# Four edits to the issue order of a four-branch encoder layer: a time-step load as one row, head weights split tile by tile, one attention stage in source order, U weights loaded ahead

## The chip, the cores and the metric

The kernel runs on one core of one Trainium2 chip. The metric is the device time of one execution in microseconds (us). The core has five engines with instruction streams of their own: TensorE (PE in the rows; its weight loads are PEld), VectorE (DVE), ScalarE (ACT), GpSimd (POOL) and SyncE (SP), which here only issues DMAs. Each engine takes its instructions strictly in their order and waits at semaphores for the others. ACT and POOL can issue DMAs too.

## The reference, cut to what matters

One residual layer over x (2048 tokens, 1024 channels), all in float32. One input projection feeds four branches; each branch is gated by a SiLU path, projected, and merged by sigmoid gates before one output projection.

```python
h = rms_norm(x, norm_g)
proj = einsum('bsd,dc->bsc', h, w_in)                 # 1024 x 10240
a_out = s5_branch(ssm_u, ..., log_dt, ...)            # diagonal state space; dt = exp(log_dt), 32 groups
b_out = retention(q, k, v)                            # 4 heads, chunks of 64
c_out = diff_attention(q, k, v)                       # 4 heads, two softmaxes each, blocks of 128 queries
m_out = memory_attention(q, mem)                      # 4 heads, 256 memory tokens
x = x + (sum_n sigmoid(merge_n + b_n) * (branch_n * silu(gate_n)) @ w_branch_n) @ w_out
```

## The kernel before

The sequence is worked in two blocks of 1024 tokens, `b` = 0 and 1. Each block runs these stages one after the other: retention (`retention_branch`; in block 0 its `side` also holds the norms of x, the S5 tables and the memory keys), differential attention (`diff_branch`), the Strassen-like projections (`projections`), merge, and output. In the trace, retention of block 0 runs from about 30 to 370 us, its attention to 680, its projections to 1160, merge and output to 1510; block 1 takes the rest.

A float32 product is made of three float32r matmuls (`mm3`, L74 to L76): weights and activations are split into a high part (a cast on ACT, names ending in h) and a low part (a subtraction on POOL or DVE, names ending in l). The splits of weights are thus work for ACT, POOL and DVE that has to be ready when PE wants it. `load_w512` loads and splits the eight 128x512 tiles of one head's query, key, value and gate weights, `w5h` and `w5l`; even tiles are subtracted on POOL, odd ones on DVE. The raw tiles `w_r` have four buffers.

Inside retention and attention the order of the work is written with `Events`: each step of each unit (a head `h` and a tile `t` of 128 tokens, 32 units for each block) gets a time in units, and the steps are emitted sorted by that time. A Tile scheduler then reorders the emitted instructions on each engine by its own estimate of when they are ready, with the emitted order as priority. One unit of attention passes through `queries`, `score` (PE scores, DVE maximum, ACT exponential `pr`), `weights_a` and `weights_b` (the coefficients `cf`), `mix` (DVE, and ACT for odd chunks, combine the two softmaxes into one `pr`), `turn` (PE transposes of `pr` into `tr`, an ACT copy to `at`), `values` (PE, `o<-vt,at`), `finish` (an ACT scaling `on` by `rms_r`, which POOL computes) and `store`. The projection of a unit that comes `lead` units later is spread between them in eight steps of three matmuls. In the last `lead` units, where no projection is left, `tail` puts the projection of the S5 input U there instead (`s5_input`): four column tiles `e`, each with weights of two 128x512 pieces that are loaded and split (`w1h`, `w1l`) at the start of its first half.

In retention a unit is `project`, `scale`, `turn`, `score` (PE, then DVE masks into `rsm`), `values` (PE, L919 to L922), `finish` and `store`.

The first DMAs of the program are, on SP, `n_x` (x, tile 0), `n_g` (the norm's gain, spread to all partitions), `n_x` (tile 1), four `w_r`, `rdec`, `n_x` (tile 2), four more `w_r`; and, on ACT, two that bring `log_dt` into `ldt`, whose source pattern steps over every second float:

```python
A.dma_start(out=ldt[g2 * 64:(g2 + 1) * 64, :],
            in_=bass.AP(src.tensor, src.offset + g2, [[0, 64], [2, NPAIR]]))
```

`ldt` is needed by `setup_s5` alone, whose first step is `dt` on POOL.

Of the kernel before, what the change touches and what calls it, by code (L numbers as in the profile page):

```python
# [15 lines left out]
ALU = mybir.AluOpType  # L16
# [27 lines left out]
def trunk_kernel(ctx, tc, a):  # L44
    nc = tc.nc
    V, A, G, PE, DMA = nc.vector, nc.scalar, nc.gpsimd, nc.tensor, nc.sync

# [94 lines left out]
    def setup_vectors(p):  # L142
# [18 lines left out]
        V.tensor_scalar(HEAD_G, HEAD_G, 0.5 * (1.0 - LAMBDA_INIT), None, op0=ALU.mult)  # L161
        lt = p.tile([128, 4, 64], F32, name="lt")
# [284 lines left out]

    def raw_w128(src):
# [187 lines left out]
    def diff_branch(b, wp, close_w, tail):  # L636
# [6 lines left out]
        with pool("diff", side="right") as p:  # L643

            def project(h, t):
                st = heads[h]
                if t == 0:
                    st["w"] = w_in512(wp, DQ_C, h)
# [20 lines left out]
                yield from proj_nat(o, b, t, st["w"])  # L669
# [153 lines left out]
            dense = []  # L823

            def start_tail():
                close_w()
                dense.append(tail())

            for i, u in enumerate(units):
# [8 lines left out]
                for c in range(n):  # L838
                    at(i + 1.22 + lag + 0.9 * c / n, x.mix, c)
                    at(i + (1.57, 1.52)[b] + lag + 0.9 * c / n, x.turn, c)  # L840
                    at(i + (1.85, 1.77)[b] + lag + 0.9 * c / n, x.values, c)
                at(i + 2.8 + lag, x.finish)
                if x.t % 4 == 3:
                    at(i + 3.3 + lag, x.store)
# [17 lines left out]
    class Ret:  # L862


        w, raws = {}, {}
# [4 lines left out]
        def project(self):  # L870
            b, h, t, p = self.b, self.h, self.t, self.p
            if t == 0:
# [6 lines left out]
            yield from proj_nat(o, b, t, Ret.w[h])  # L879
# [64 lines left out]
    def retention_branch(b, wp, side):  # L944
        with pool("ret") as p, ExitStack() as wx2:
# [6 lines left out]
            for i, (h, t) in enumerate((h, t) for h in range(NH) for t in range(8)):  # L952
# [5 lines left out]
                events.at(i + 3.3, x.values)  # L958
                events.at(i + 4.1, x.finish)
                if t % 4 == 3:  # L960
                    events.at(i + 4.7, x.store)
# [6 lines left out]
    def s5_input(b, e, w1, up):  # L968
# [610 lines left out]
    for b in range(NBLK):  # L1579
# [4 lines left out]
        if b == 0:  # L1584
            with ExitStack() as sx:
# [116 lines left out]
```

## Time and profile before

| what | value |
|---|---|
| runs | 3047.42, 3050.52, 3054.89 us, median 3050.52 us |
| the profiled execution | 3045.78 us, span of its instructions 3043.5 us |
| PE busy | 2899.1 us, 95% of the span |
| DVE, ACT, POOL busy | 1920.5, 1332.3, 1247.0 us |
| granted clock of TensorE, mean | 0.99 |
| moved by DMA | 351.75 MB |

The profiled execution is 4.7 us below the median. A busy PE is not PE at its peak: a matmul counts as busy until its modelled end, which overlaps the next one. An idle time is put down to the engine and the line that ended it.

### The profile page before, as it was taken

Reading aid. Unit: us, or ns where it says so; the run is one execution under the profiler, and the core shown is the slowest. Engines: PE = TensorE matmul, PEld = TensorE weight load, DVE = VectorE, ACT = ScalarE, POOL = GpSimd, SP = SyncE. Lnnn points to the kernel's source line nnn. Section 1 sums busy time; section 2 is a strip of 40 time slices with the busy share of each in tenths; the row PEclk is TensorE's granted clock in tenths of the full one; section 3 lists DMA queues with packets and bytes.
Section 4 is the critical chain, followed back from the end, with each engine's and each line's share of the span. In section 5 each row is a group of like instructions: output and inputs, shape, how many; then the busy total and the mean of one; then the engine's idle time right before and its main releaser. Section 6 shows DMA issues by size and latency. Waiting matters only on the chain. (4 is left out here: it accounts for less than half of the span.)

```text
span 3043.5 us, 43500 instructions
## 1 busy us (share of the span) xinstructions
PE 2899.1 (95%) x14514; PEld 2381.9 (78%) x14514; DVE 1920.5 (63%) x4613; ACT 1332.3 (44%) x3357; POOL 1247.0 (41%) x1157
## 2 busy tenths in 40 slices
PE   5999999998999999999999999999999999999999
PEld 4777877777888888777788878878878888887777
DVE  5885587766655545656544378888766555446654
ACT  3323355563333344423433257767733333444332
POOL 2543533334444442555132242232244444434560
PEclk9999999999999999999999999999999999999999
DMA  5332422233444436555521220120134444355653
GB/s 154 97 92 77 126 68 68 68 97 119 141 150 142 134 109 204 188 182 175 161 69 43 63 66 22 58 61 21 59 115 142 144 142 137 125 184 166 194 167 96
DMA packets 319341, 351.75 MB, mean 116 GB/s; under 512 B 28479, under 2 KB 238478, under 8 KB 319118
## 3 DMA queue, kind: packets, MB, share of 16 engines
q1 hardware_dynamic: 314734, 340.59, 35.7%
q0 software_dynamic: 2304, 8.39, 0.9%
q8 instruction: 114, 1.87, 0.3%
q14 instruction: 109, 0.89, 0.1%
q10 hardware_dynamic: 2080, 0.01, 0.0%
HBM read 247.98 MB, written 100.93 MB: 115 GB/s over the span
## 5 line engine op out<-in xcount | busy, mean ns | idle before, releaser
L1294 POOL TENSOR_TENSOR p_l<-p_r,p_h 128x512 fp32r<-128x512 f32 x260 | 368.4, 1420 | 458.3 <-ACT p_h L1293 445.3
L74 PE MATMUL mm<-w5h,xh 128*128 128x512 f32 x1024 | 436.3, 426 | 17.9 <-ACT xh L577 16.5
L75 PE MATMUL mm<-w5l,xh 128*128 128x512 f32 x1024 | 406.7, 397 | 3.5 <-POOL w5l L443 3.5
L76 PE MATMUL mm<-w5h,xl 128*128 128x512 f32 x1024 | 406.9, 397 | 0.0
L138 POOL TENSOR_TENSOR rms_r<-rms_m,mhalf 128x1 f32<-128x1 f32 (+1 forms) x228 | 179.0, 787 | 488.2 <-DVE rms_m L136 422.6
L1293 ACT CAST p_h<-p_r 128x512 fp32r<-128x512 f32 x260 | 160.3, 621 | 376.6 <-PE mm L1332 85.8
L758 ACT ACTIVATE pr<-sc,nm 128x512 f32<-128x512 f32 (+3 forms) x320 | 200.1, 626 | 148.0 <-DVE nm L756 146.4
L74 PEld LDWEIGHTS mm<-w5h,xh 128*128 128x128 f32 x1024 | 195.2, 191 | 48.3 <-ACT xh L577 16.9
L76 PEld LDWEIGHTS mm<-w5h,xl 128*128 128x128 f32 x1024 | 194.2, 190 | 43.9
L75 PEld LDWEIGHTS mm<-w5l,xh 128*128 128x128 f32 x1024 | 195.8, 191 | 32.1 <-POOL w5l L443 4.7
L75 PE MATMUL sc<-br_l,w1h 128*128 128x512 f32 x496 | 197.3, 398 | 6.9 <-DVE br_l L1212 6.9
L74 PE MATMUL sc<-br_h,w1h 128*128 128x512 f32 x496 | 200.5, 404 | 3.3 <-DVE mg_g L1265 3.3
L756 DVE TENSOR_REDUCE nm<-sc 128x1 f32<-128x512 f32 (+3 forms) x320 | 193.2, 604 | 9.3 <-PE sc L752 5.1
L76 PE MATMUL sc<-br_h,w1l 128*128 128x512 f32 x496 | 197.3, 398 | 0.0
L1266 POOL TENSOR_TENSOR mg<-mg,mg_g 128x512 f32<-128x512 f32 x96 | 140.9, 1471 | 91.9 <-DVE mg_g L1265 83.8
L806 PEld LDWEIGHTS o<-vt,at 128*128 128x128 f32 x1088 | 142.4, 193 | 38.0 <-ACT at L799 29.6
L806 PE MATMUL o<-vt,at 128*128 128x128 f32 x1088 | 152.0, 279 | 16.6 <-ACT at L799 16.5
L460 POOL TENSOR_TENSOR w1l<-w_r,w1h 128x512 fp32r<-128x512 f32 x86 | 119.4, 1401 | 113.3 <-ACT w1h L459 95.8
L443 POOL TENSOR_TENSOR w5l<-w_r,w5h 128x512 fp32r<-128x512 f32 x72 | 96.0, 1336 | 109.9 <-ACT w5h L442 73.7
L1332 PE MATMUL mm<-xh,p_h 128*128 128x512 f32 x336 | 134.0, 399 | 0.3 <-ACT p_t L1402 0.3
L1332 PE MATMUL sc<-xl,p_h 128*128 128x512 f32 x336 | 131.6, 392 | 2.7 <-DVE xl L1367 2.7
L1332 PE MATMUL sc<-xh,p_h 128*128 128x512 f32 x336 | 131.3, 391 | 0.6 <-ACT p_h L1293 0.6
(396 smaller groups left out, 7653.6 us busy)
## 6 DMA issues: line engine op xcount, KB each, us to landing
p_r<-in_w_in SPq DMA_DIRECT2D x88, 512.0 KB
w_r<-in_w_in SPq DMA_DIRECT2D x144, 256.0 KB
me_d<-p_t SPq DMA_DIRECT2D x128, 256.0 KB
mg_g<-me_d SPq DMA_DIRECT2D x64, 512.0 KB
s_m<-mats_d SPq DMA_DIRECT2D x32, 640.0 KB
w_r<-in_w_branch SPq DMA_DIRECT2D x64, 256.0 KB
w_r<-br SPq DMA_DIRECT2D x64, 256.0 KB
n_x<-in_x SPq DMA_DIRECT2D x16, 512.0 KB
```

The costliest lines, as they stand in the source:

```text
L74: PE.matmul(out, l[0], r[0], start=first, stop=False)
L75: PE.matmul(out, l[0], r[1], start=False, stop=False)
L76: PE.matmul(out, l[1], r[0], start=False, stop=last)
L138: G.tensor_tensor(r, m, mhalf[:, 0:n], op=ALU.pow)
L460: G.tensor_tensor(lo, raw, hi.bitcast(F32), op=ALU.subtract)
L756: V.tensor_reduce(nm, s[:, 0:n], axis=AX.X, op=ALU.max, negate=True)
L758: A.activation(e[:, 0:n], s[:, 0:n], AF.Exp, bias=nm, accum_out=self.zz[:, m, c:c + 1])
L806: PE.matmul(self.o[:, 0:128], self.at[c][:, q * 128:(q + 1) * 128], self.st["vts"][c][:, q, :], start=c == 0 and q == 0, stop=c * 4 + q == ...
L1266: G.tensor_tensor(dst, dst, t, op=ALU.add)
L1293: A.copy(hi, x)
L1294: G.tensor_tensor(lo, x, hi.bitcast(F32), op=ALU.subtract)
L1332: PE.matmul(o, l[:, k, :], r, start=first and k == 0 and q == 0, stop=k == 3 and q == 2, skip_group_check=True)
```

## The change

1. `log_dt` is loaded as one contiguous row of 32 floats, spread to all partitions, by an SP DMA in `setup_vectors` (after the first x tiles and weights), and two DVE copies pick the even and the odd entries into `ldt`. The two ACT DMAs at the program's start go.
2. `w512_steps` splits a head's weights one tile for each step, within the last projection steps of the head before (and, in attention, the first of its own head), in place of `w_in512` in one piece at the head's first tile. The first head of each stage, and in block 1 retention's first head, still load in one piece.
3. The whole attention stage of block 0 (`events.run()` with b = 0) is issued on DVE, ACT, POOL and PE in the order of the source, without the scheduler's reordering. Block 1 is still scheduled.
4. U weights: the pieces of column tile e + 1 are requested when tile e begins and split after its first half; those of tile 0 are requested 0.7 unit before the tail and split when it begins. The tail's steps come three eighths of a unit later.
5. Some times in `Events` move: attention's `values` from 1.85 to 1.95 (block 0) and 1.77 to 1.82 (block 1), `finish` and `store` a little later; retention's `values` from 3.3 to 3.6, `finish` from 4.1 to 4.4, `store` from 4.7 to 5.0.

```diff
@@ setup_vectors
+        row = p.tile([128, NPAIR, 2], F32, name="ldt_r")
+        DMA.dma_start(out=row.rearrange("p j g -> p (j g)"), in_=a["ssm_log_dt"][0].partition_broadcast(128))
+        for g2 in range(2):
+            V.tensor_copy(ldt[g2 * 64:(g2 + 1) * 64, :], row[g2 * 64:(g2 + 1) * 64, :, g2])
@@ new
+    def w512_steps(p, src, w):
+        raws = [raw_w512(src, k) for k in range(4)]
+        yield
+        for k in range(8):
+            raw = raws.pop(0)
+            hi = p.tile([128, 512], F32R, name="w5h", bufs=8)
+            lo = p.tile([128, 512], F32R, name="w5l", bufs=8)
+            A.copy(hi, raw)
+            (V if k % 2 else G).tensor_tensor(lo, raw, hi.bitcast(F32), op=ALU.subtract)
...
+            if k < 4:
+                raws.append(raw_w512(src, k + 4))
+            yield
@@ diff_branch, project
-                if t == 0:
-                    st["w"] = w_in512(wp, DQ_C, h)
+                if t == 7 and h + 1 < NH:
+                    heads[h + 1]["w"] = [], []
+                    heads[h + 1]["ws"] = w512_steps(wp, cols512(DQ_C, h + 1), heads[h + 1]["w"])
...
-                yield from proj_nat(o, b, t, st["w"])
+                groups = proj_nat(o, b, t, st["w"])
+                for k in range(8):
+                    if t == 0 and h and k < 5:
+                        next(st["ws"])
+                    if t == 7 and h + 1 < NH and k in (1, 5, 6, 7):
+                        next(heads[h + 1]["ws"])
+                    next(groups, None)
+                    if k < 7:
+                        yield
@@ diff_branch, events
-                    at(i + (1.85, 1.77)[b] + lag + 0.9 * c / n, x.values, c)
+                    at(i + (1.95, 1.82)[b] + lag + 0.9 * c / n, x.values, c)
...
+                        at(i - 0.7, lambda: ahead.append([raw_u(0, k) for k in range(2)]))
                         at(i, start_tail)
                     for k in range(8):
-                        at(i + (k + 0.5) / 8, lambda: next(dense[0], None))
-            events.run()
+                        at(i + (k + 3.5) / 8, lambda: next(dense[0], None))
+            with ExitStack() as ox:
+                if b == 0:
+                    ox.enter_context(tc.manual_schedule(engines=ORDERED))
+                events.run()
@@ Ret.project
-                if h or b:
-                    Ret.w[h] = w_in512(self.wps[h % 2], RQ_C, h, Ret.raws.pop(h, ()))
+                if h == 0 and b:
+                    Ret.w[h] = w_in512(self.wps[0], RQ_C, h, Ret.raws.pop(h, ()))
...
+                if t == 6 and k == 1 and h + 1 < NH:
+                    Ret.w[h + 1] = [], []
+                    Ret.ws = w512_steps(self.wps[(h + 1) % 2], cols512(RQ_C, h + 1), Ret.w[h + 1])
+                    next(Ret.ws)
+                if t == 7 and h + 1 < NH:
+                    next(Ret.ws)
@@ retention_branch
-                events.at(i + 3.3, x.values)
+                events.at(i + 3.6, x.values)
@@ s5_input
-        w = w_in128(w1, U_C + e * 128)
+        w = ws.pop(e)
+        if e < 3:
+            raws = [raw_u(e + 1, k) for k in range(2)]
...
+            if hf == 0 and e < 3:
+                ws[e + 1] = s5_weights(w1, raws)
@@ block 0, before the norms
-                for g2 in range(2):
-                    src = a["ssm_log_dt"]
-                    A.dma_start(out=ldt[g2 * 64:(g2 + 1) * 64, :],
-                                in_=bass.AP(src.tensor, src.offset + g2, [[0, 64], [2, NPAIR]]))
```

The order of instructions shows what moves. First POOL at the start of the program, where `dt` stood ahead of the first split of weights. Before:

```order
L138 TENSOR_TENSOR rms_r<-rms_m,mhalf 128x1
L194 TENSOR_TENSOR dt<-ebase,ldt 128x16
L443 TENSOR_TENSOR w5l<-w_r,w5h 128x512
L138 TENSOR_TENSOR rms_r<-rms_m,mhalf 128x1
L443 TENSOR_TENSOR w5l<-w_r,w5h 128x512
```

And in the changed program, the same engine from the same place on:

```order
L139 TENSOR_TENSOR rms_r<-rms_m,mhalf 128x1
L448 TENSOR_TENSOR w5l<-w_r,w5h 128x512
L139 TENSOR_TENSOR rms_r<-rms_m,mhalf 128x1
L448 TENSOR_TENSOR w5l<-w_r,w5h 128x512
L139 TENSOR_TENSOR rms_r<-rms_m,mhalf 128x1
L448 TENSOR_TENSOR w5l<-w_r,w5h 128x512 x2
L943 TENSOR_TENSOR rqk<-ram,rbm 128x256
L139 TENSOR_TENSOR rms_r<-rms_m,mhalf 128x1
L943 TENSOR_TENSOR rqk<-ram,rbm 128x256
L199 TENSOR_TENSOR dt<-ebase,ldt 128x16
L207 TENSOR_TENSOR mag<-ebase,t_872 128x16
L175 TENSOR_TENSOR ls<-eb,ls 128x2
```

`dt` has moved behind the first splits and the first two retention units, to just ahead of `mag`.

Second ACT in block 0's attention, where the weights of the second head are split. Before:

```order
L442 CAST w5h<-w_r 128x512 x2
L799 COPY at<-tr 128x512
L442 CAST w5h<-w_r 128x512
L758 ACTIVATE pr,zz<-sc,nm 128x256
L442 CAST w5h<-w_r 128x512
L629 ACTIVATE ho_j,ho_ss<-o 128x128
L442 CAST w5h<-w_r 128x512
L740 CAST qh<-tr 128x256
L633 ACTIVATE on<-on,rms_r 128x128
L442 CAST w5h<-w_r 128x512
L799 COPY at<-tr 128x128
L442 CAST w5h<-w_r 128x512
```

In the changed program, the same place:

```order
L829 COPY at<-tr 128x512
L788 ACTIVATE pr,zz<-sc,nm 128x256
L650 ACTIVATE ho_j,ho_ss<-o 128x128
L770 CAST qh<-tr 128x256
L461 CAST w5h<-w_r 128x512
L788 ACTIVATE pr,zz<-sc,nm 128x256
L829 COPY at<-tr 128x128
L461 CAST w5h<-w_r 128x512 x2
L701 COPY raw<-mm 128x256
L702 COPY vt<-mm 128x128
L632 ACTIVATE si_t<-mm 128x128
L654 ACTIVATE on<-on,rms_r 128x128
```

Six casts stood ahead of the small `at` copy, and `on` with them; now one cast does, and `on` comes behind the copy.

Third PE at that same unit: from the transpose of `pr` to the product `o<-vt,at` that uses its copy. Before:

```order
L797 MATMUL tr<-ident,pr 128x128
L74 MATMUL mm<-w5h,xh 128x512
L75 MATMUL mm<-w5l,xh 128x512
L76 MATMUL mm<-w5h,xl 128x512
L74 MATMUL mm<-w5h,xh 128x512
L75 MATMUL mm<-w5l,xh 128x512
L76 MATMUL mm<-w5h,xl 128x512
L806 MATMUL o<-vt,at 128x128
```

In the changed program:

```order
L827 MATMUL tr<-ident,pr 128x128
L75 MATMUL mm<-w5h,xh 128x512
L76 MATMUL mm<-w5l,xh 128x512
L77 MATMUL mm<-w5h,xl 128x512
L75 MATMUL mm<-w5h,xh 128x512
L76 MATMUL mm<-w5l,xh 128x512
L77 MATMUL mm<-w5h,xl 128x512
L75 MATMUL mm<-w5h,xh 128x512
L76 MATMUL mm<-w5l,xh 128x512
L77 MATMUL mm<-w5h,xl 128x512
L836 MATMUL o<-vt,at 128x128
```

One more group of three projection matmuls now stands between the transpose and its use.

## Rows read from the trace of the kernel before

**Rows 1.** Stretches: PE, PEld, DVE, ACT, POOL busy us, granted clock, DMA share, GB/s.

```profile
500.00:600.00 100.00, 92.94 (x511) 76.67 (x510) 79.73 (x245) 57.41 (x182) 39.39 (x57) 1.00 0.21 65
900.00:1000.00 100.00, 100.00 (x488) 81.81 (x487) 52.59 (x108) 39.09 (x67) 43.75 (x33) 1.00 0.47 151
```

**Rows 2.** Timeline of the start: start us, us, what [idle before it <- releaser].

```profile
2.26 19.86 SPq L432 DMA_DIRECT2D w_r<-in_w_in  x4
4.32 1.06 ACT L565 ACTIVATE n_junk<-n_x 128x1024 bf16<-128x1024 f32 x1 [0.80 <-DMA n_x<-in_x]
26.15 1.06 ACT L565 ACTIVATE n_junk<-n_x 128x1024 bf16<-128x1024 f32 x1 [20.68 <-DMA n_x<-in_x]
26.50 2.91 POOL L194 TENSOR_TENSOR dt<-ebase,ldt 128x16 f32<-128x16 f32 x1 [20.20 <-DMA ldt<-in_ssm_log_dt]
29.25 0.62 ACT L442 CAST w5h<-w_r 128x512 fp32r<-128x512 f32 x1 [0.22 <-DMA w_r<-in_w_in]
29.38 1.27 POOL L443 TENSOR_TENSOR w5l<-w_r,w5h 128x512 fp32r<-128x512 f32 x1
30.41 0.79 PE L74 MATMUL mm<-w5h,xh 128*128 128x512 f32 x1 [16.50 <-ACT xh L577]
34.73 1.12 PE L574 MATMUL tr<-ident,n_x 128*128 128x128 f32 x4 [3.10 <-DVE xl L578]
```

**Rows 3.** DMA queues: 0 to 40 us, then 10 to 15 us (q10 ACT's, q1 SP's): packets, MB, share.

```profile
q10 hardware_dynamic: 2080, 0.01, 2.4%
...
q10 hardware_dynamic: 547, 0.00, 4.8%
q1 hardware_dynamic: 3, 0.00, 0.2%
```

**Rows 4.** Stretches of the start and of slow clocks, columns as in rows 1.

```profile
2.00:4.00 2.00, 0.00 (x0) 0.00 (x0) 0.30 (x1) 1.28 (x1) 0.00 (x0) 1.00 0.83 252
36.00:40.00 4.00, 4.00 (x17) 3.38 (x16) 3.92 (x4) 2.57 (x5) 3.21 (x3) 1.00 1.04 338
102.50:106.00 3.50, 3.50 (x10) 2.43 (x9) 3.35 (x12) 1.14 (x4) 2.02 (x2) 0.51 0.71 212
460.00:464.40 4.40, 3.88 (x12) 3.21 (x13) 3.12 (x11) 2.92 (x11) 2.08 (x3) 0.61 0.86 260
2130.00:2150.00 20.00, 16.84 (x86) 13.62 (x86) 14.80 (x39) 11.43 (x31) 8.54 (x9) 0.91 0.34 106
```

**Rows 5.** Waits of PE, 40 to 110, then 60 to 380 us: us in total, times, longest.

```profile
PE tr L574 <- DVE rms_m L136: 2.7, 1, 2.7
...
PE sc L919 <- DVE rsm L911: 5.4, 5, 3.0
```

**Rows 6.** Waits of PE from 380 to 740 us (attention, block 0, and after).

```profile
PE o L806 <- ACT at L799: 12.5, 15, 3.0
...
PE tr L797 <- DVE kt L714: 3.0, 4, 1.3
PE tr L797 <- DVE sc L754: 1.9, 4, 0.5
```

**Rows 7.** Timeline of the longest of these waits: ACT, then PE.

```profile
459.39 0.40 ACT L633 ACTIVATE on<-on,rms_r 128x128 f32<-128x128 f32 x1 [1.02 <-POOL rms_r L138]
460.21 0.26 ACT L799 COPY at<-tr 128x128 f32<-128x128 f32 x1
...
460.51 0.49 PE L806 MATMUL o<-vt,at 128*128 128x128 f32 x2 [3.00 <-ACT at L799]
```

**Rows 8.** Waits of PE: 1790 to 2260 us (attention, block 1), then 2120 to 2150 us.

```profile
PE o L806 <- ACT at L799: 4.0, 7, 0.7
...
PE mm L76 <- POOL w1l L460: 0.6, 1, 0.6
...
PE tr L797 <- DVE pr L790: 2.9, 2, 2.5
```

**Rows 9.** Waits of PE from 1480 to 1790 us (retention, block 1), the first.

```profile
PE mm L75 <- POOL w5l L443: 3.5, 3, 2.3
```

More of the change, by code (lines that the diff above doesn't have):

```diff
@@ L46, in trunk_kernel @@
     V, A, G, PE, DMA = nc.vector, nc.scalar, nc.gpsimd, nc.tensor, nc.sync
+    ORDERED = {x.engine for x in (V, A, G, PE)}
     def pool(name, bufs=1, side=None, space=None):
@@ L446, in load_w512 @@
         return his, los
+    def w512_steps(p, src, w):
[7 more added lines that the diff above has]
+            (V if k % 2 else G).tensor_tensor(lo, raw, hi.bitcast(F32), op=ALU.subtract)
+            w[0].append(hi)
+            w[1].append(lo)
+            if k < 4:
+                raws.append(raw_w512(src, k + 4))
+            yield
     def raw_w128(src):
@@ L633, in head_scale, with diff_branch @@
         A.mul(on, on, r)
-    def diff_branch(b, wp, close_w, tail):
+    def diff_branch(b, wp, close_w, tail, ahead):
         nkv, npr = ((4, 12), (6, 14))[b]
@@ L823, in diff_branch @@
             dense = []
+            heads[0]["w"] = w_in512(wp, DQ_C, 0)
             def start_tail():
@@ L827, in start_tail @@
                 dense.append(tail())
+                next(dense[0])
             for i, u in enumerate(units):
@@ L862, in trunk_kernel @@
     class Ret:
-        w, raws = {}, {}
+        w, raws, ws = {}, {}, None
         def __init__(self, b, h, t, wps, p, rtab, rmask):
@@ L875, in project @@
                     DMA.dma_start(out=state[h], in_=state_d[:, h, :])
-                if h or b:
-                    Ret.w[h] = w_in512(self.wps[h % 2], RQ_C, h, Ret.raws.pop(h, ()))
+                if h == 0 and b:
+                    Ret.w[h] = w_in512(self.wps[0], RQ_C, h, Ret.raws.pop(h, ()))
             o = ps_mm()
-            yield from proj_nat(o, b, t, Ret.w[h])
+            groups = proj_nat(o, b, t, Ret.w[h])
+            for k in range(8):
+                if t == 6 and k == 1 and h + 1 < NH:
[4 more added lines that the diff above has]
+                    next(Ret.ws)
+                next(groups, None)
+                if k < 7:
+                    yield
             qk = o[:, 0:256].rearrange("p (a d) -> p a d", a=2)
@@ L957, in retention_branch @@
                 events.at(i + 2.7, x.score)
-                events.at(i + 3.3, x.values)
-                events.at(i + 4.1, x.finish)
+                events.at(i + 3.6, x.values)
+                events.at(i + 4.4, x.finish)
                 if t % 4 == 3:
-                    events.at(i + 4.7, x.store)
+                    events.at(i + 5.0, x.store)
                 if i == 6:
@@ L965, in retention_branch, with raw_u, s5_weights, s5_input @@
             events.run()
-    def s5_input(b, e, w1, up):
-        w = w_in128(w1, U_C + e * 128)
+    def raw_u(e, k):
+        return raw_w128(w_in[k * 512:(k + 1) * 512, U_C + e * 128:U_C + (e + 1) * 128])
+    def s5_weights(w1, raws):
+        return [load_w128(w1, None, raw, bufs=4) for raw in raws]
+    def s5_input(b, e, ws, w1, up):
+        w = ws.pop(e)
+        if e < 3:
+            raws = [raw_u(e + 1, k) for k in range(2)]
         us = up.tile([128, 8, 128], F32, name="us", bufs=1)
@@ L1636, in tail @@
             with pool("us") as up:
+                ws = {0: s5_weights(w1, ahead.pop(0))}
+                yield
                 for e in range(4):
@@ L1639, in tail @@
                         ahead[0].load()
-                    yield from s5_input(b, e, w1, up)
-        dense = diff_branch(b, wp, wx.close, tail)
+                    yield from s5_input(b, e, ws, w1, up)
+        dense = diff_branch(b, wp, wx.close, tail, ahead)
         drain(dense)
```

4 lines of the change are left out of this document (2 added, 2 removed).

## Prediction, made before the changed kernel ran

> **What bounds the kernel now.** I read the stretches of 100 us first, because an average over stages says little here. In the projections PE is busy for the whole stretch; in attention of block 0 it is idle for 7 of 100 us while no other engine is full [rows 1]. PE busy 2899.1 us of a span of 3043.5 us leaves about 144 us of PE idle in the whole program, and that is all that a change of order can win directly; nothing here shortens a matmul. So the question for each edit is which of PE's waits it ends, and I read PE's waits stage by stage.
>
> The largest is at the start. PE's first projection matmul comes at 30.41 us after an idle time of 16.50 us [rows 2]. It hangs on ACT, which stood 20.68 us for `n_x` (tile 1), a transfer that SP had requested before 2.26 us. The reader is to see three things together: SP needed 19.86 us to issue four `w_r` [rows 2]; from 10 to 15 us ACT's queue sent 547 packets and SP's three [rows 3]; and POOL's `dt`, which waits for `ldt` itself, began at 26.50 us, right after `n_x` had come [rows 2]. The 2,080 packets of `ldt` carry 0.01 MB [rows 3]. I take it that this load, one packet for each float, holds up everything queued beside it until it is through.
>
> A second fact makes long waits dearer: after the wait of 3.00 us at 460.51 us [rows 7] the granted clock of the stretch is 0.61, a mixture of 2.4 and 1.2 GHz, and after the 3.0 us wait in retention it is 0.51 [rows 4, 5]. A stretch at half clock loses half its length: 4.4 x 0.39 = 1.7 us and 3.5 x 0.49 = 1.7 us.
>
> **The start (edit 1).** With `ldt` gone, what has to land before the first matmul after tile 0 (landed at 4.32 us [rows 2]) is `n_g` and `n_x` of 512 KB each and four `w_r` of 256 KB: 2048 KB, 2.10 million bytes. SP's loads moved 252 GB/s before `ldt` began to count, and 338 GB/s later [rows 4]: 8.3 or 6.2 us, so the last `w_r` lands at 12.6 or 10.5 us. Before, the first matmul followed the start of the fourth cast, which waited for that `w_r`, by 30.41 - 29.25 = 1.16 us [rows 2]. It comes at 13.8 or 11.7 us, 16.6 or 18.7 us earlier. Beyond that, POOL's first `w5l` had to stand behind `dt` until 29.38 us, and the second four `w_r` could be requested only when it was done; the 3.10 us wait at 34.73 us [rows 2] follows from this crowding and may go too. Bounds 16.6 to 21.8; I take **-17**, because the wait at 34.73 is for DVE, whose own list is unchanged.
>
> The new row load is one more SP issue after the first weights; it is wanted by `dt` alone. But `dt`'s 2.91 us of POOL [rows 2] now lie ahead of `mag`, `ls` and the norms' `rms_r`, in a place where PE already waited 2.7 us for that chain [rows 5], and on DVE two copies and the product with `dt` stand ahead of an `xl`. Between 0 and 2.9 us; I take half, **+1.5**.
>
> **Retention, block 0 (edits 2 and 5).** PE waits 5.4 us in five places for `rsm` (DVE) before `values` [rows 5], and one of them brings 1.7 us of half clock. `values` comes 0.3 of a unit later, two groups of three projection matmuls by the order. A stretch of attention holds 511 matmuls in 100 us [rows 1], so a matmul is some 0.2 us apart from the next (an estimate) and six give 1.2 us. That covers the four shorter waits, which hold 2.4 us, and shortens the 3.0 us one, perhaps below the point where the clock falls. Bounds 0 to -7.1; I take **-5**. The splits of heads' weights cost nothing here either way: the waits for `w5l` are 3.5 us in block 1's retention and all belong to its first head, which still loads in one piece [rows 9]: **0**.
>
> **Attention, block 0 (edits 2, 3 and 5).** 12.5 us in 15 waits of `values` for the `at` copy [rows 6]. The longest shows why: the small copy at 460.21 us had stood on ACT behind casts of the next head's weights and behind `on`, which itself stood 1.02 us for POOL's `rms_r` [rows 7], and POOL was splitting the same weights. In the changed order one cast stands ahead of this copy, `on` behind it, and PE has one more group of three matmuls, some 0.6 us, to work on first. The longest is gone twice over; most others are below 1 us, the size of what the later time gives. With the half clock after the longest the bounds are 0 and -14.2; I take **-10**. The source order also moves ACT's and DVE's share of `mix`. The transposes' waits of 3.0 and 1.9 us [rows 6] could shrink by that or double, so 4.9 us either way; I take **0**.
>
> **Attention, block 1, and both tails (edits 4 and 5).** Block 1's `values` waits hold 4.0 us [rows 8], and 0.05 of a unit is about 0.7 us there, as long as the longest of them. Between 2120 and 2150 us the transposes wait 2.9 us for `pr`, 2.5 of it at once [rows 8], while POOL splits two U pieces at a time and DVE waits for POOL; the clock of that stretch, 0.91 over 20 us [rows 4], costs 1.8 us. Splitting the pieces half a column tile ahead takes this apart. Together 0 to -8.3; I take **-5**. The waits for `w1l` of 0.6 us [rows 8], in each block one: **-1**.
>
> **The sum.** -17 + 1.5 - 5 - 10 - 5 - 1 = -36.5 us against the profiled execution: 3045.8 - 36.5 = **3009 us**. That execution lies 4.7 us below the median of the runs, so the same gain from the median would give 3014; I stay with the profiled sum, since a PE that waits less should also vary less, and put the difference into the range. All bounds at their best give 3045.8 - 21.8 - 7.1 - 14.2 - 4.9 - 8.3 - 1.2 = 2988; the start at its least, `dt` at its dearest, nothing else gained and the transposes worse give 3045.8 - 16.6 + 2.9 + 4.9 = 3037.
>
> **The rivals.** *The start stays slow.* It could be that `ldt` is only the visible queue and SP's loads crawl for a reason of their own, the spread of `n_g` for instance. Its packets take 2.4% of 16 engines over 40 us [rows 3], under 1 us of their time, which speaks for this rival; against it stands that SP's queue stood still just as long as these packets ran, and not after. Then the start's 17 us stay and the result is 3009 + 17 = 3026. The Trainium skill ("DMA: Bandwidth & Descriptors", section "SWDGE vs HWDGE vs iDMA") says that each DMA engine goes round-robin between its queues and switches at packet boundaries; by that rule SP's packets should have slipped in between ACT's and the load would cost about nothing. The trace disagrees: three packets of SP in 5 us.
>
> *The order wins nothing.* The waits for `at` only move to the next operation: `values` comes later, then `on`, the stores and the next unit's buffers come later too, and PE stands for these instead. For it: each unit's chain is as long as before. Against it: in that stage ACT and POOL are idle more than 40 of 100 us [rows 1], so later work finds room. Then the start alone counts: 3045.8 - 17 + 1.5 = 3030.
>
> *Slower.* In source order an engine that waits holds everything behind it, and nothing is pulled forward past the wait. The place would be ACT's part of `mix` and `on` in block 0's attention: ACT's product for odd chunks now stands behind the `at` copy, DVE's sum waits for it, and the next scores' maxima wait behind DVE. To be slower by 0.3% (9 us) the 32 units must lose 36.5 + 9 = 45.5 us and more, 1.4 us each; in the 16 units with two chunks 2.8 us each, nearly the longest wait of before [rows 6] every time. DVE is the fullest engine there, 80 of 100 us [rows 1], so it isn't excluded. It would give 3055 or more.
>
> *The edits of order do harm and just eat the start's gain:* 15 us of new waits in the same place, 3045 or so.
>
> **How the numbers follow.** The case I hold likeliest has 0.75, its own range 2988 to 3023. The start staying slow 0.05, the order winning nothing 0.13, the gain eaten 0.04, slower 0.03. The range of 8 in 10 takes in the first three up to 3034, with its lower end where all bounds are at their best: 2988 to 3034. A difference of 0.3%, 9 us, is about what a measurement of this kernel can tell from none. Faster by more than that: 0.75 + 0.05 + 0.13 = 0.93; within 0.04; slower 0.03.
>
> **What would show it.** Right: the first L75 matmul of the changed kernel (L74 before) between 11 and 14.5 us, ACT's wait for `n_x` a few us, no queue with thousands of tiny packets; PE's waits for `at` in block 0's attention down to a few us, and no clock below 0.9 in a stretch around its second head; the wait for `rsm` nearly gone; the transposes near the end of block 1's attention without a wait above 1 us. Wrong: a first matmul after 25 us; or PE's waits for DVE's `pr` or for `kt` in block 0's attention above 10 us, which would say that the source order holds DVE up.

## The result, and the profile after

The changed kernel is slower: 3082.91 us median (3082.18 to 3087.04) against 3048.97 us (3043.69 to 3054.89) for the kernel before in the same session, a ratio of 1.0117 with a 95% interval of 1.0103 to 1.013. The forecast was 3009 us. The profiled execution took 3082.93 us, its span is 3081.0 us, 37.5 us more than before. The table splits these 37.5 us. Its ends are starts of matmuls, read from the timelines: the first projection matmul, the first score (L751 before, L781 after), block 0's last `o<-vt,at`, the first matmul of the S5 scan (`o<-s_u,s_m`), block 1's first score and its last `o<-vt,at`.

| stretch | before | after | difference | forecast |
|---|---|---|---|---|
| start, to the first projection matmul | 30.4 | 12.8 | -17.6 | -17 |
| retention, block 0, to the first score | 339.6 | 345.9 | +6.3 | -5 + 1.5 |
| attention, block 0, first score to last value matmul | 302.6 | 356.5 | +53.9 | -10 |
| from there to the first matmul of the S5 scan | 67.4 | 69.7 | +2.3 | -1, both blocks |
| from there to block 1's first score | 1022.0 | 1022.3 | +0.3 | 0 |
| attention, block 1, first score to last value matmul | 449.2 | 447.0 | -2.2 | -5, with the next |
| from there to the end | 832.3 | 826.8 | -5.5 | |

So one stage lost three times what the start won. First the start as it is now, from the timeline (start us, us, what, idle before it), to be read against [rows 2]:

```profile
2.13 2.37 SPq L437 DMA_DIRECT2D w_r<-in_w_in  x4
...
7.88 1.06 ACT L586 ACTIVATE n_junk<-n_x 128x1024 bf16<-128x1024 f32 x1 [2.41 <-DMA n_x<-in_x]
...
12.85 0.80 PE L75 MATMUL mm<-w5h,xh 128*128 128x512 f32 x1 [2.98 <-ACT xh L598]
```

SP needs 2.37 us for the four `w_r` where it needed 19.86, and ACT waits 2.41 us for tile 1 where it waited 20.68. PE's wait of 16.50 us ahead of its first projection matmul is now 2.98.

Next the stages, as stretches of before (columns as in [rows 1]): retention of block 0 and its attention.

```profile
30.40:370.00 339.60, 317.03 (x1639) 255.76 (x1640) 242.96 (x774) 117.26 (x342) 155.03 (x158) 0.98 0.39 110
370.00:672.60 302.60, 282.93 (x1517) 232.85 (x1516) 227.63 (x690) 172.76 (x533) 115.13 (x160) 0.99 0.24 75
```

The same of the changed kernel, behind the two stretches of [rows 1]:

```profile
500.00:600.00 100.00, 82.14 (x422) 64.40 (x421) 68.13 (x203) 47.73 (x155) 30.79 (x49) 0.98 0.17 55
900.00:1000.00 100.00, 100.00 (x494) 82.04 (x493) 51.87 (x105) 39.71 (x68) 44.63 (x34) 1.00 0.45 146
12.80:358.80 346.00, 323.27 (x1639) 260.43 (x1640) 251.41 (x775) 115.84 (x342) 151.43 (x156) 0.97 0.38 109
358.80:715.30 356.50, 300.92 (x1519) 236.37 (x1518) 237.22 (x691) 172.42 (x533) 109.01 (x162) 0.97 0.20 62
```

The projections are untouched (PE busy for all of 900 to 1000 us). In the attention stretch the work is the same (1517 and 1519 matmuls, 533 instructions of ACT), but PE is idle for 356.5 - 300.92 = 55.6 us where it was idle for 19.7, and its busy time grew by 18 us while the clock fell from 0.99 to 0.97. From 500 to 600 us DVE is busy 68 us where it was busy 80 [rows 1], ACT 48 where it was 57, POOL 31 where it was 39: every engine does less. That looks like engines that wait for each other in a ring, not like one that is full.

What PE waits for there (380 to 785 us, against [rows 6]):

```profile
PE o L836 <- ACT at L829: 26.4, 23, 2.2
PE tr L827 <- DVE pr L820: 15.2, 15, 1.8
```

The waits for `at`, which were to shrink from 12.5 us, have doubled, and those for `pr` have appeared. Who makes ACT and DVE late is seen in their own waits in that stretch (358 to 716 us), DVE first:

```profile
DVE gate L633 <- ACT si_t L632: 30.8, 24, 1.8
DVE ql L771 <- ACT qh L770: 20.0, 18, 2.4
DVE rms_m L137 <- ACT ho_j L650: 18.3, 31, 0.9
...
ACT pr L788 <- DVE nm L786: 129.1, 91, 4.0
```

The kernel before has in the same stage (370 to 673 us) next to none of the first three, and half of the last:

```profile
ACT pr L758 <- DVE nm L756: 57.7, 44, 3.2
...
DVE rms_m L136 <- ACT ho_j L629: 4.4, 9, 1.2
...
DVE ql L741 <- ACT qh L740: 2.4, 8, 0.5
```

How such a wait runs on is seen in the timeline of the changed kernel between 529 and 538 us, DVE first:

```profile
529.04 0.69 DVE L786 TENSOR_REDUCE nm<-sc 128x1 f32<-128x512 f32 x1
530.84 0.43 DVE L771 TENSOR_TENSOR ql<-tr,qh 128x256 fp32r<-128x256 f32 x1 [1.11 <-ACT qh L770]
...
533.20 0.69 DVE L786 TENSOR_REDUCE nm<-sc 128x1 f32<-128x512 f32 x1
535.35 0.29 DVE L633 SCALAR_TENSOR_TENSOR gate<-si_t,mm 128x128 f32<-128x128 f32 x1 [1.46 <-ACT si_t L632]
...
536.72 0.16 DVE L797 TENSOR_TENSOR nm<-nx,nm 128x4 f32<-128x4 f32 x1
```

ACT in the same time, and the two PE rows around its last copy:

```profile
529.76 0.69 ACT L788 ACTIVATE pr<-sc,nm 128x512 f32<-128x512 f32 x1 [1.06 <-DVE nm L786]
...
530.44 0.36 ACT L770 CAST qh<-tr 128x256 fp32r<-128x256 f32 x1
...
533.92 0.69 ACT L788 ACTIVATE pr<-sc,nm 128x512 f32<-128x512 f32 x1 [2.11 <-DVE nm L786]
...
535.01 0.30 ACT L632 ACTIVATE si_t<-mm 128x128 f32<-128x128 f32 x1
...
536.91 0.21 ACT L798 ACTIVATE cf<-nm 128x4 f32<-128x4 f32 x1 [1.30 <-DVE nm L797]
537.02 0.46 ACT L829 COPY at<-tr 128x384 f32<-128x384 f32 x1
...
533.19 0.52 PE L827 MATMUL tr<-ident,pr 128*128 128x128 f32 x3
537.54 0.71 PE L836 MATMUL o<-vt,at 128*128 128x128 f32 x4 [1.55 <-ACT at L829]
```

DVE gives ACT a maximum (533.20) and then stands at `gate`, whose `si_t` is on ACT behind the exponential of that maximum; ACT runs exponential, copies and `si_t`, then stands at `cf`, whose `nm` is on DVE behind `gate` and four more. The two take turns. The transposes had been done at 533.71 us, but their copy stands behind all of this on ACT and runs at 537.02, and PE waits 1.55 us. The Trainium skill ("PSUM — Partial Sum Buffer", section "Engine vs sequencer instructions") says that the queues of ScalarE and VectorE are strict FIFO; this trace agrees, with a copy ready at 533.71 us that runs 3.3 us later.

### The profile page after: what moved, and what is told of

It reads as the page before. It is cut to its first block, busy times and chain, and to the rows that moved or that the text cites. A ratio compares the mean times of both kernels' runs of the same rounds, so it can differ in the third digit from the quotient of the medians.

```text
span 3081.0 us, 43507 instructions
## 1 busy us (share of the span) xinstructions
PE 2915.2 (95%) x14514; PEld 2389.5 (78%) x14514; DVE 1937.1 (63%) x4615; ACT 1335.2 (43%) x3357; POOL 1240.2 (40%) x1157
## 5 line engine op out<-in xcount | busy, mean ns | idle before, releaser
L1350 POOL TENSOR_TENSOR p_l<-p_r,p_h 128x512 fp32r<-128x512 f32 x260 | 361.9, 1395 | 455.7 <-ACT p_h L1349 452.6
L786 DVE TENSOR_REDUCE nm<-sc 128x1 f32<-128x512 f32 (+3 forms) x320 | 193.0, 605 | 12.6 <-PE sc L782 8.3
L1388 PE MATMUL mm<-xh,p_l 128*128 128x512 f32 x336 | 131.0, 390 | 0.0
L1388 PE MATMUL sc<-xh,p_l 128*128 128x512 f32 x336 | 130.8, 389 | 0.0
```

The costliest lines, as they stand in the source:

```text
L786: V.tensor_reduce(nm, s[:, 0:n], axis=AX.X, op=ALU.max, negate=True)
L1350: G.tensor_tensor(lo, x, hi.bitcast(F32), op=ALU.subtract)
L1388: PE.matmul(o, l[:, k, :], r, start=first and k == 0 and q == 0, stop=k == 3 and q == 2, skip_group_check=True)
```

## The experiments

The same stretches in every kernel, and its ratio to the kernel before in its own session. "Long attention" reaches from the first score to the first matmul of the S5 scan, so it doesn't depend on how the tail is laid over the last units.

| kernel | ratio, 95% interval | retention, block 0 | attention, block 0 | long attention |
|---|---|---|---|---|
| before | 1 | 339.6 | 302.6 | 370.0 |
| changed | 1.0117 (1.0103 to 1.013) | 345.9 | 356.5 | 426.2 |
| e1 no source order | 0.9954 (0.9937 to 0.997) | 348.7 | 305.3 | 367.9 |
| e2 before + source order | 1.0237 (1.0218 to 1.0256) | 340.1 | 384.2 | 448.1 |
| e3 before + edit 1 | 0.9939 (0.9917 to 0.9961) | 339.5 | 303.3 | 371.2 |
| e4 values later | 1.0078 (1.0063 to 1.0094) | 347.4 | 346.5 | 416.1 |
| e5 ACT in source order | 0.9933 (0.9915 to 0.995) | 345.2 | 299.6 | 367.9 |
| e6 DVE | 0.9923 (0.9909 to 0.9938) | 345.9 | 299.5 | 367.1 |
| e7 PE | 0.9961 (0.9946 to 0.9976) | 346.6 | 307.2 | 375.2 |
| e8 e1, retention's times of before | 0.9924 (0.9905 to 0.9943) | 347.1 | 305.0 | 367.7 |
| e9 ACT and DVE | 1.0085 (1.0067 to 1.0103) | 347.7 | 348.9 | 417.3 |
| e10 ACT and PE | 0.9956 (0.9938 to 0.9974) | 345.5 | 307.5 | 375.2 |
| e11 DVE and PE | 0.9944 (0.9922 to 0.9966) | 344.8 | 308.3 | 375.9 |
| e12 ACT, DVE and PE | 1.0104 (1.0081 to 1.0127) | 347.3 | 353.9 | 422.2 |
| e13 three DVE parts later | 1.0024 (1.0012 to 1.0036) | 351.9 | 320.8 | 388.6 |
| e14 gate's part later | 1.0114 (1.0096 to 1.0131) | 349.0 | 352.9 | 423.4 |
| e15 e1, retention's weights whole | 0.9944 (0.9926 to 0.9961) | 346.8 | 304.7 | 366.2 |
| e16 e6, retention's weights whole | 0.9927 (0.9913 to 0.9942) | 347.2 | 299.2 | 367.5 |
| e17 ql and head's root later | 1.0009 (0.9999 to 1.0019) | 348.8 | 325.4 | 392.9 |
| e18 e16, retention's times of before | 0.9917 (0.9902 to 0.9931) | 341.9 | 299.3 | 367.3 |

**Which edit.** e1 takes edit 3 out of the changed kernel, e2 puts it alone into the kernel before, e3 puts edit 1 alone there, e4 moves the value matmuls.

```diff
@@ e1 (e2 has the two lines the other way round, in the kernel before)
-                if b == 0:
-                    ox.enter_context(tc.manual_schedule(engines=ORDERED))
@@ e4
-                    at(i + (1.95, 1.82)[b] + lag + 0.9 * c / n, x.values, c)
+                    at(i + (2.25, 1.82)[b] + lag + 0.9 * c / n, x.values, c)
...
```

> The changed kernel without edit 3: block 0's attention is ordered by the scheduler again, everything else as changed. Theory 'held queues' (in source order an instruction that waits holds all that stands behind it on its engine; the stretch from the first score matmul to the last value matmul of block 0 grew from 302.6 to 356.5 us by it): that stretch comes back to 295 to 305 us and the time to 3020 to 3032 us. Rival 'split weights' (the loss comes from the pieces of the head weights between the projection's groups, edit 2): the stretch stays above 340 us and the time above 3065 us.

> The kernel before with edit 3 alone. 'Held queues': the same stretch grows by 54 us or more, since the head weights then stand in one piece in the source order too; time 3095 to 3120 us. 'Split weights': no change, 3045 to 3052 us.

> The kernel before with edit 1 alone (the time steps as one row). The first matmul of the projection stands at about 12.9 us as in the changed kernel (30.41 before). If nothing is given back later the time is 3031 us; if the retention stage of block 0 owes its 6.3 us (339.6 to 345.9 us from the first projection matmul to the first score) to the new start, as by the dt arithmetic that now lies beside the first norms, 3037 us; if that loss comes from the later values of edit 5 or from the split weights, 3031 us.

> The changed kernel with the value matmuls of block 0's attention 0.3 unit later in the list (1.95 to 2.25, with finish and store behind them). 'Held queues' with ACT's copies of the turned tiles (at) as the place: PE's waits for at (28 us over the program, 26.4 of them in block 0) fall below 8 us, and the time falls by 15 to 25 us to 3057 to 3067 us. If the chain that counts is another (DVE's sums for the transposes, 24.6 us of PE's waits), the wait moves there and the time stays within 8 us of 3081 us.

e1: the stretch is 305.3 us, 0.3 above what was expected; the loss is gone with the source order, and "split weights" falls for this stage. Its median of 3038.46 us lies above the expected 3020 to 3032. The attention stretch of e1, to compare with the changed kernel's 358.80:715.30 (PE idle 23.4 us for 55.6, clock 0.99 for 0.97):

```profile
361.50:666.80 305.30, 281.90 (x1509) 233.30 (x1509) 227.05 (x691) 173.61 (x533) 116.68 (x160) 0.99 0.23 73
```

Of the 51 us between the two kernels, 32 are idle time of PE and 19 are its busy time. The stretches at 1.2 GHz add up to 20.6 us in the changed kernel and 6.8 in e1, which by half explains 7 of the 19 us; the rest of the 19 is not taken apart.

e2 lost more than expected, 81.6 us in the stretch: with the head weights in one piece the casts stand in the source order too, so the split weights and the other moved times do help, but only against a harm that the source order makes; which of them helps is not taken apart. e3 wins 18 us of span; its median of 3034.18 us lies between the two times expected, but its retention stage is 339.5 us: the new start owes nothing later, and the 6 to 9 us lost in retention belong to another edit. e4 fell between its two cases. The value matmuls' waits for `at` no longer show from 358 to 716 us (27.7 us there in the changed kernel), but 10 us of 51 came back, and the transposes wait more for `pr`, 21.4 us for 15.2:

```profile
PE tr L827 <- DVE pr L820: 21.4, 22, 1.9
```

So PE's wait for `at` is where the delay is felt, not where it is made.

**Which engines.** Seven kernels differ from the changed one in the set of engines that is held to the source order; the rest is left to the scheduler.

```diff
-    ORDERED = {x.engine for x in (V, A, G, PE)}
+    ORDERED = {x.engine for x in (A,)}
```

(e5; in e6 (V,), in e7 (PE,), in e9 (V, A), in e10 (A, PE), in e11 (V, PE), in e12 (V, A, PE).)

> The changed kernel with ACT alone held to the source order in block 0's attention; DVE, POOL and PE are ordered by the scheduler. The stretch from the first score to the last value matmul is 356.5 us with all four in source order and 305.3 us with none (e1). Theory 'ACT's queue' (the copy of the turned tiles stands behind an exponential or the exponential of the coefficients, which wait for DVE): at least 30 of the 51 us come back, 335 us or more, and PE's waits for at are above 15 us. Theory 'DVE's queue': under 315 us here. Theory 'jointly' (each engine's fixed place hurts only because the others are fixed too): 310 to 330 us here and for DVE and PE alone.

> The changed kernel with DVE alone held to the source order in block 0's attention. 'DVE's queue' (sums for the transposes and the maxima for the exponentials stand behind the projection's epilogue, so PE waits for pr and ACT for nm): the stretch is 335 us or more, with PE's waits for pr above 15 us. 'ACT's queue': under 315 us. 'Jointly': 310 to 330 us.

> The changed kernel with PE alone held to the source order in block 0's attention. Rival 'PE's own queue' (value matmuls and transposes that wait hold the projection's matmuls behind them): the stretch is 335 us or more. 'ACT's queue' and 'DVE's queue': under 315 us, since ACT and DVE then run the copies and sums as they come ready. 'Jointly': 310 to 330 us.

> The changed kernel with ACT and DVE held to the source order in block 0's attention, PE and POOL ordered by the scheduler. One engine alone in source order cost nothing (e5 299.6 us, e6 299.5, e7 307.2 from the first score to the last value matmul, against 305.0 to 305.3 with none). Theory 'ACT and DVE hold each other' (in the changed kernel ACT waits some 121 us for DVE's maxima, DVE some 28 us for ACT's gate and 18 us for ACT's qh, each with other work behind): the stretch is 335 us or more. Rival 'PE must be fixed too' (a scheduled PE puts projection matmuls where the copies are late, so late copies cost nothing): 298 to 312 us.

> The changed kernel with ACT and PE held to the source order in block 0's attention. 'PE must be fixed too', with ACT's copy as the place: the stretch is 335 us or more and PE's waits for at are above 15 us. 'ACT and DVE hold each other': 298 to 312 us.

> The changed kernel with DVE and PE held to the source order in block 0's attention. If DVE's fixed order with PE's is the place: 335 us or more, with PE's waits for pr above 15 us. 'ACT and DVE hold each other': 298 to 312 us.

> The changed kernel with ACT, DVE and PE in source order in block 0's attention and POOL alone ordered by the scheduler. If POOL's fixed order is no part of the loss: 350 to 360 us for the stretch and a time within 8 us of the changed kernel's, 1.009 to 1.014 of before. If POOL's queue (the root of the norms, POOL's rms_r, behind the rotation and the low halves) is part: 340 us or less.

e5 to e7: no single engine's order costs what was expected of it, and "ACT's queue", "DVE's queue" and "PE's own queue" all fall; "jointly" had named too high a price for one engine. e9 to e11 find the pair: ACT with DVE 348.9 us, ACT with PE 307.5, DVE with PE 308.3. e12 leaves POOL little: 4 us of long attention (426.2 against 422.2). Long attention nearly adds up: a fixed ACT and DVE cost 417.3 - 367.9 = 49 us, a fixed PE 7 to 8 us (375.2, 375.2 and 375.9), together 57 of the 58.3 us that the changed kernel loses to e1.

How DVE alone can be fixed without harm is seen in the waits of e6 (358 to 716 us), DVE in source order and ACT scheduled:

```profile
DVE rms_m L137 <- ACT ho_j L650: 26.9, 32, 2.1
DVE gate L633 <- ACT si_t L632: 2.4, 4, 1.0
DVE ql L771 <- ACT qh L770: 1.9, 3, 1.4
...
ACT pr L788 <- DVE nm L786: 41.0, 50, 2.4
```

ACT's list is then built around DVE's: by the waits, `qh` and `si_t` mostly stand where DVE wants them, though `ho_j` does not (26.9 us). In e9 both lists are fixed, and the waits are those of the changed kernel, though PE, which is free, waits 7.5 us for `at` there and 3.0 for `pr`:

```profile
DVE gate L633 <- ACT si_t L632: 29.6, 23, 1.8
DVE rms_m L137 <- ACT ho_j L650: 19.1, 32, 1.0
DVE ql L771 <- ACT qh L770: 18.5, 19, 1.9
...
ACT pr L788 <- DVE nm L786: 131.0, 93, 3.6
...
PE o L836 <- ACT at L829: 7.5, 10, 1.6
PE tr L827 <- DVE pr L820: 3.0, 5, 1.3
```

**Which instructions of the two.** e13 keeps the source order on all four engines and moves three DVE parts later in the list, away from the ACT instruction that they need; e14 moves the first part alone, e17 the other two alone. Nothing of the computation changes.

```diff
@@ e13, e14: gate, square and root of the projection, out of project's last step
+                if b == 0:
+                    at(i - lead + 1.2, epilogue, *u)
...
@@ e13, e17: the subtraction of ql, out of queries
                 at(i - 0.35, x.queries)
+                if b == 0:
+                    at(i - 0.15, x.low)
...
@@ e13, e17: the root of the head's norm, out of values
+                if b == 0:
+                    at(i + 2.1 + lag + 0.9 * (n - 1) / n, x.root)
...
```

> The changed kernel, all four engines in source order, but in block 0's attention three DVE parts stand later in the list than the ACT instruction that they need: gate, square and root of the projection 0.26 unit after its last matmul (1.2 units after its start), ql 0.2 unit after qh, the head's root 0.15 unit after ho_j. Theory 'DVE stands waiting for ACT just ahead, ACT then for DVE's maxima': DVE's waits for si_t, qh and ho_j in that stretch (28.3, 18.5 and 18.4 us) fall below 20 us together, ACT's waits for nm fall from 121 to under 90 us, and the stretch falls from 356.5 to 330 us or less. Rival 'the maxima and exponentials hold each other': the three waits go, the stretch stays at 345 us or more.

> As e13, but with the projection's part alone (gate, square and root) later. If the gate's wait for si_t (28.3 us, the longest of the three) is the place: at least two thirds of what e13 gains. If the three share the loss by their waits: 28.3 of 65.2, some 40 per cent of it. Rival: the stretch stays at 345 us or more.

> The changed kernel, all four engines in source order, with ql 0.2 unit and the head's root 0.15 unit later in block 0's attention, and the projection's part (gate, square, root) where the changed kernel has it. Theory 'ql and the head's root hold the loss' (a wait on the path from score to score; the gate's is not on it): the stretch from the first score to the last value matmul is 320 to 327 us, as in e13 (320.8). Rival 'only together' (what one wait gives back, the next takes): 340 us or more, and it takes all three.

e13 brings 35.7 us back, and the three waits fall to 8.9 us together. e14 brings 3.6, a tenth of that: for the gate alone the rival was right, and both shares expected of it were too large. e17 brings 31.1, as expected from its first theory, and the kernel is as fast as before (1.0009). The waits of e17 (358 to 716 us):

```profile
DVE gate L633 <- ACT si_t L632: 24.3, 19, 1.5
DVE ql L776 <- ACT qh L770: 3.7, 4, 1.1
DVE rms_m L137 <- ACT ho_j L849: 3.6, 6, 0.6
...
ACT pr L793 <- DVE nm L791: 96.2, 87, 2.4
...
PE o L841 <- ACT at L834: 9.7, 12, 1.5
PE tr L832 <- DVE pr L825: 8.9, 11, 1.4
```

The longest of the three waits, the gate's, is mostly still there (24.3 of 30.8 us) and nearly harmless. The two that go are each shorter (20.0 and 18.3 us). PE is idle for 32.6 us in e17 and 32.8 in e13; the 4.6 us between the two stretches are PE's busy time, at a mean granted clock of 0.98 and 1.00. So the timeline from 529 to 538 us above, with the gate in it, shows how a delay is handed on, not which wait costs. Some 20 us of the loss stay in e17 (325.4 against 305.3 us in e1); what holds them is not shown. One expectation failed: ACT's waits for `nm` fell only from 129.1 to 118.3 us in e13, so their sum doesn't measure the harm either. `ql` and the root were not taken apart from each other. Neither wait harms by itself where the other engine is scheduled: e6 has 26.9 us of the root's, e5 12.6 us of `ql`'s, and the stretch is 299.5 and 299.6 us.

**The retention stage.** e8, e15 and e18 ask for the 6 to 9 us lost there. e8 and e15 are e1 with one of its two retention edits undone; e16 and e18 have DVE alone in source order, with one and both undone.

```diff
@@ e8, e18
-                events.at(i + 3.6, x.values)
+                events.at(i + 3.3, x.values)
...
@@ e15, e16, e18
-                if h == 0 and b:
-                    Ret.w[h] = w_in512(self.wps[0], RQ_C, h, Ret.raws.pop(h, ()))
+                if h or b:
+                    Ret.w[h] = w_in512(self.wps[h % 2], RQ_C, h, Ret.raws.pop(h, ()))
...
```

> The changed kernel without edit 3 (as e1) and with the retention stage's times of before (values 3.3, finish 4.1, store 4.7: the retention's part of edit 5 undone). From the first projection matmul to the first score before and e3 have 339.5 us, e1 348.7, the changed kernel 345.9. Theory 'later values' (the state's chain and the matmuls wait for what now stands later): the stretch comes back to 338 to 342 us and the time to 0.992 to 0.993 of before. Rival 'split weights' (the pieces of the head weights, four raw tiles loaded at once, lie among DVE's and POOL's setup work): it stays at 345 us or more, and the time at e1's 0.9954.

> e1 (no source order) with the retention's head weights of block 0 and 1 in one piece again; the retention's later values stay. Theory 'split weights' for the retention stage: from the first projection matmul to the first score it comes back from 345 to 348 us to 340 us or less, to about 335 us if the later values win the 5 us that the prediction gave them; time 0.991 to 0.993 of before. If the stage stays at 345 us or more with the weights whole and the times later, the two edits would each cost alone and not add.

> The best parts seen: DVE alone in source order in block 0's attention (e6: 299.5 us there) and the retention's head weights in one piece (e15). If the gains add: 0.989 to 0.991 of before; if the retention's weights don't matter: e6's 0.992.

> As e16 (DVE alone in source order in block 0's attention, the retention's head weights in one piece) with the retention's times of before too, so that its stage is that of e3. If the two retention edits cost alone and don't add: 339 to 341 us from the first projection matmul to the first score (e16 347.2), with TensorE's mean granted clock in it at 0.98 again, and 0.989 to 0.991 of before in all. If the stage's time hangs on something else in the changed kernel: 345 us or more and e16's 0.9927.

"Later values" fell with e8 (347.1 us), "split weights" with e15 (346.8): undoing either changes little, undoing both brings 341.9 us, a little over the 339 to 341 expected. e8's ratio, 0.9924, is the one that "later values" had named, but the profiled spans of e8 and e1 are 3026.2 and 3025.5 us, so it says nothing for that theory. e16 came at e6's ratio, as if the weights did not matter. The 13 kernels with both retention edits spread over 344.8 to 351.9 us here, e8, e15 and e16 over 346.8 to 347.2, and those with neither (before, e2, e3, e18) over 339.5 to 341.9. The stage as one stretch in e8, e15 and e18 (12.6 and 12.8 us on), one row of each kernel:

```profile
12.60:359.70 347.10, 323.83 (x1639) 261.10 (x1640) 241.36 (x776) 117.22 (x342) 153.71 (x157) 0.96 0.38 107
```

```profile
12.80:359.60 346.80, 323.36 (x1639) 260.86 (x1640) 249.16 (x776) 115.16 (x342) 152.41 (x157) 0.97 0.38 107
```

```profile
12.80:354.70 341.90, 318.37 (x1639) 257.83 (x1640) 242.75 (x775) 117.50 (x342) 153.40 (x156) 0.98 0.39 110
```

With before (339.60) and changed (346.00) above, all five have 1639 matmuls and 22.6 to 23.5 us of PE idle. The whole difference is PE's busy time, 317 to 324 us, and it goes with the granted clock, 0.98 to 0.96. So PE's waits did not grow in sum; PE ran longer at the lower level. Added up by the profile's clock, the stretches at 1.2 GHz in this stage are 10 us before and 24 in the changed kernel; half of the extra 14 us is 7, for 6.2 us of busy time. Over all twenty kernels they run from 6.8 to 30.7 us, and PE's busy time goes with them, from 316 to 326 us. The longest such place in the changed kernel:

```profile
150.00:156.00 6.00, 4.39 (x30) 3.21 (x29) 5.92 (x15) 1.66 (x7) 3.73 (x4) 0.99 0.34 89
156.00:166.00 10.00, 10.00 (x36) 6.86 (x35) 8.61 (x39) 2.44 (x7) 1.99 (x2) 0.50 0.60 167
```

PE waited 1.6 us there for DVE's `ca` of the S5 setup (L419), was busy 4.39 of 6 us, and then ran 10 us at 1.2 GHz, which by half of it costs 5 us. The wait alone does not decide it: e11 has the same 1.6 us wait for `ca` at 154.8 us and its clock stays at 1.00 until 166 us, and e8 has its 10 us at 0.50 (196 to 206 us) after a wait of only 0.84 us. In all three the matmuls around it are the setup's transposes of `ca` (L419). Why either edit alone brings such places stays open; that the scheduler lays the setup's work around the retention steps, which both edits shift, is likely but not shown.

**The best order.** e18 is the fastest seen, 0.9917 (0.9902 to 0.9931), some 25 us under the kernel before. It is edit 1, edits 2, 4 and 5 in the attention, and DVE alone in source order. Its interval overlaps those of e3, e6, e8 and e16, so what it has over edit 1 alone (0.9939) is not settled.

## Why the prediction was wrong, step by step

**The start** was right, in its mechanism too: 12.85 us against 11.7 to 13.8, with the fourth cast at 11.69 us and the first matmul 1.16 us behind it as before, and 18 us in e3, where nothing else changed. `dt`'s new place showed: PE's wait for `sn` of 4.2 us in the same place took over from the 2.7 us wait [rows 5], the +1.5 that was put in. That the size came out so well is luck, as it was taken as half of a range of 2.9. And the stage didn't grow by it: e3 has a wait of 4.1 us there and still 339.5 us, because the 3.10 us wait for `xl` [rows 2], which the -17 left as it was, is 1.5 us in e3 (1.4 in the changed kernel). The row of `sn`, and that of `rsm` for the next step:

```profile
PE tr L595 <- DVE sn L191: 4.2, 1, 4.2
...
PE sc L965 <- DVE rsm L957: 1.3, 3, 0.8
```

The rival "the start stays slow" fell. By the round-robin rule of the Trainium skill ("DMA: Bandwidth & Descriptors", section "SWDGE vs HWDGE vs iDMA") removing a load of 0.01 MB would have won about nothing; the trace disagrees, with 18.0 us of span between e3 and before. Whether SP's packets themselves or the issuing of its loads was held is not shown.

**Retention, -5**: the wait for `rsm` did fall, from 5.4 [rows 5] to 1.3 us. The step forgot that later steps also move the setup's work (PE's waits for its `gm` are 6.9 us from 60 to 380 us, 3.7 before, and 7.0 in e15, which has the later values without the split), and that TensorE's clock answers: 6.2 us more of PE's busy time for the same matmuls. The sign was wrong. The 0 for the split weights was wrong too: with the values where they were before, e8 loses as much.

**Attention, block 0, -10, and the transposes, 0**: this is the step that failed: +53.9 us against -10. It looked at one unit's copy and what stood ahead of it on ACT, on one engine at a time, and that reading was true: fewer casts do stand ahead. What it left out is that with ACT and DVE both fixed each has instructions whose partner stands just ahead on the other (`nm` and exponential, `qh` and `ql`, `ho_j` and the root), and that the scheduler, not the list of the kernel before, had kept such pairs apart: the waits for `ho_j` and `qh` are 4.4 and 2.4 us before and 18.3 and 20.0 after. e2 shows it: the old list in source order has 15.6 and 21.6 us of them (370 to 756 us). What was put at nothing is thus the price of fixing both engines at once, 44 us in e9 (348.9 against 305.3 in e1). It also took idle shares for room ("ACT and POOL are idle more than 40 of 100 us"); ACT is idle more now, and late. Even without edit 3 the -10 was too much: e1 has 7.0 us of waits for `at` in place of 12.5 [rows 6], and long attention is 2.1 us shorter than before.

**The rival "slower"** had the right mechanism ("in source order an engine that waits holds everything behind it") and its threshold was passed: 1.4 us per unit below the forecast, measured 53.9 + 10 = 63.9 us in this stretch, 2.0 per unit. Its place was wrong: DVE's wait for ACT's part of `mix` is 8.7 us in 7 waits between 380 and 780 us, less than any of the three above. It was given 0.03, and weighed as one operation in some of the units, not as a property of two queues. The sign that the prediction named for this case, waits for `pr` above 10 us, is there: 15.2 us. The rivals "the order wins nothing" and "the gain eaten" fell, as neither has more than 15 us of new waits.

**Block 1's attention and the tails, -5**: the values' waits are gone there (0.3 us for 4.0), but the transposes wait 9.3 us for `pr`, once for 2.5, as much as before (9.0, once 2.5), and new waits of 6.2 us for `ob` came. The rows of the changed kernel from 1835 to 2300 us, for [rows 8]:

```profile
PE tr L827 <- DVE pr L820: 9.3, 5, 2.5
PE tr L766 <- ACT ob L641: 6.2, 6, 1.3
...
PE o L836 <- ACT at L829: 0.3, 1, 0.3
```

The stretch is 2.2 us shorter and the rest 5.5. The 20 kernels, whose code there is that of before or of the change, spread over 445 to 450 us and 825 to 836 us in these two. Added, the two take 1279 to 1285 us in the three with the code of before and 1272 to 1283 in the 17 with that of the change, 14 of these under 1277 and 5.9 us less in the mean. So the forecast of -5 is probably about right in size, but no run has edits 4 and 5 alone there, and the rows show only the values' waits gone. Edit 5's 0.05 unit did what was forecast of it; edit 4 did not end the transposes' long wait.

## What to carry to other kernels

Fixing the order of one engine cost nothing here for ACT and DVE, and 7 us of long attention for PE, while the others were still laid around it; fixing two that exchange products in both directions (ACT and DVE, 49 us of it) is another change, and has to be costed as one: list each consumer that stands just behind its producer's turn on the other engine. When every engine is less busy than before in a stage that has become longer, look for such a pair, and test it by freeing one engine at a time, then by pairs. A wait does not cost by its length: moving the gate's 30.8 us, the longest of three, brought 3.6, moving the other two, 38.3 us together, brought 31.1.

## What the runs showed of the hardware

TensorE's clock can cost more than the wait ahead of it: 1.6 us of waiting, then 10 us at 0.50 (156 to 166 us), 5 us lost; but in e11 the same wait was followed by none of it. The two stretches of slow clock in [rows 4] lost 1.7 us each, after waits of 3 us. In the retention stage of block 0 the difference between the five kernels shown, 317 to 324 us of PE's busy time for 1639 matmuls, goes with the time at 1.2 GHz, as it does in all twenty.
